# A two-layer decoder trunk on one core: the first pair of tiles of each feed-forward by eight plain products, the sums of input blocks made beside them

## The chip, the cores and the metric

The kernel runs on one core of a Trainium2 chip. The metric is the device time of one execution in microseconds (us); the times given are medians of several runs. TensorE (PE) multiplies, VectorE (DVE) and ScalarE (ACT) do the work element by element, GpSimd (POOL) issues the DMAs that add into their target, and SyncE (SP) issues all the others.

## The reference

512 positions of width 1024 pass through two layers. Each layer is a feed-forward, a mixer (attention and a short convolution) and a second feed-forward, so the program has four feed-forwards, called FFN1 to FFN4 here. Everything is float32. The change touches the feed-forwards alone:

```python
D_MODEL = 1024
SEQ = 512
DEPTH = 2
D_FF = 2816
...
def _swiglu(h, w1, w2):
    g, up = jnp.split(h @ w1, 2, axis=-1)
    return (jax.nn.silu(g) * up) @ w2
...
        x = x + 0.5 * gate[:, 0] * _swiglu(ada(x, 0), ffn_w1[layer, 0], ffn_w2[layer, 0])
        x = x + gate[:, 1] * _mixer(ada(x, 1), w_in[layer], q_norm_g[layer], k_norm_g[layer],
                                    conv_w[layer], conv_b[layer], w_out[layer])
        x = x + 0.5 * gate[:, 2] * _swiglu(ada(x, 2), ffn_w1[layer, 1], ffn_w2[layer, 1])
```

`ada` is an RMS norm with a scale and a shift that a linear map of `c` gives (the "ada" rows: a product of a 128x1024 weight tile with `c`, 144 of them in all, done on VectorE between other work).

## The kernel before

**Precision.** A float32 product is made of three TensorE products. Every weight tile is split into `whi` (a copy by ScalarE, L167) and `wlo` (the rest, by VectorE, L168), every input into a high and a low half (L512, L513), and `shared_bulk` (L277 to L281) issues whi·hhi, whi·hlo and wlo·hhi as matmuls of 256 columns (L280). The split weights lie in a ring of four (tags `whi`, `wlo`): a fifth split waits until the matmuls of the first are done.

**W1 by blocks.** The first matrix of a feed-forward has 22 gate tiles and 22 up tiles; they go in NP = 11 pairs, pair n being two gate tiles and two up tiles of 128 columns. The input is cut in four blocks, two halves of the sequence by two kinds of 128-row chunks (even and odd), and the weights of a pair in four blocks b11, b12, b21, b22. A plain product of a pair takes eight block products; here every pair is done by seven, numbered in the order 1, 2, 5, 6, 7, 4, 3. For that, sums are needed. Those of weight blocks are made on the way: `left` is negated by ScalarE (L215), added to by VectorE (L218, L221) and by an accumulating DMA on POOL's queue (L179). Those of input blocks, t1 to t4, are made once per feed-forward by the class `Blocks` (scale L432, shift L455, combine L473, split L512 and L513); products 5, 6, 7 and 4 need t1, t2, t3 and t4, product 3 needs the second half of the odd chunks itself. Products 1 and 2 need only the first half of the sequence. One block product is 24 matmuls: four chunks k, two tiles f, three matmuls each.

**Banks.** The results come out of PSUM by `evacuation` (L623 to L668): a copy on ScalarE (L638), additions on VectorE (L633), silu on ScalarE (L629), the product of gate and up (L648), which is split and put into the tiles `hidh`, `hidl` of a pool that opens only when the tiles of the work before are released.

**Order.** `_ffn_order` (L88) writes it out by hand: (1 and 2 of pair 0), (1 and 2 of pair 1), (2, 1), (2, 2), then 5, 6, 7 of pairs 0 and 1 in turn, (0, 4), (0, 3), (1, 4), (1, 3), then a steady pattern; W2 comes in three parts, the first after 32 block products ("the first stretch"). The steps of the input sums are queued as `steps`, each with a number of matmul columns after which it is issued (`after`, `tick`); a product that needs one not yet issued issues it first. `Feed.step` holds that loop:

```python
                while p > 2 and (p, k // 2) not in Tail.blocks[0].made:
                    steps.pop(0)[1]()
```

Weights are loaded and split ahead by `fetch`, two ahead of the product that uses them. The end of the part before a feed-forward (`Tail.run`) computes the norm of the two sequence halves one after the other, and queues `early` (the first half) and t1 to t4 (the second). FFN1 has no part before it: `side_by_side` starts it by running the four products (0,1), (0,2), (1,1), (1,2) chunk by chunk beside the ada products that give its scale and shift.

## Time and profile before

| | |
|---|---|
| time, three runs | 1901.28, 1901.44, 1902.0 us, median 1901.44 |
| the profiled execution | 1905.03 us, of which the span of the trace is 1903.2 |
| PE busy | 1832.5 us, 96% of the span |
| weight loads (PEld) | 1699.7 us, 89%, beside the matmuls |
| DVE, ACT, POOL busy | 1442.6, 944.2, 88.5 us |
| mean granted TensorE clock | 0.991 of full speed |

The profiled execution is 3.6 us longer than the median of the timed runs. In the trace, "PE" rows of L280 are the block products. A number in brackets at a row's end is the time that the engine stood idle just before that row, and behind the arrow stands what it waited for. The first L280 matmuls of the four feed-forwards start at 24.84, 618.61, 976.88 and 1552.43 us.

### The profile page before, as it was taken

To read this page: it belongs to the slowest core of one execution; us is meant where nothing else is said; L and a number is where in the kernel's file an instruction comes from. 1 tells how busy PE (TensorE), PEld (TensorE's weight loads), DVE (VectorE), ACT (ScalarE), POOL (GpSimd) and SP (SyncE) were. 2 spreads that over 40 slices of the span, in tenths; PEclk is the share of its full clock that TensorE was granted. 3 is DMA by queue.
4 is the path that set the end of the run, shared out by engine and by line. 5 is a ranking of instruction groups with operands and counts; after the bars stand their busy time and mean duration, and the time that the engine had idled before them with its cause. 6 is when DMAs were issued, how large, how long until landed. Compare 5 with 4: busy or idle time off the path is not lost.

```text
span 1903.2 us, 31033 instructions
## 1 busy us (share of the span) xinstructions
PE 1832.5 (96%) x12340; PEld 1699.7 (89%) x12340; DVE 1442.6 (76%) x2458; ACT 944.2 (50%) x1482; POOL 88.5 (5%) x164
## 2 busy tenths in 40 slices
PE   4899999999999899999989999999999998999999
PEld 3898999999888898998889999898998898989898
DVE  7896887787866997878779777866977768647564
ACT  4652543446664752542565435344656656436342
POOL 0100000000000000000001000000000001000000
PEclk9899999999999999999999999999999999999999
DMA  8687785522314488777607866723222327626422
GB/s 336 188 242 256 207 244 176 155 76 71 102 67 133 98 247 266 194 229 240 211 23 212 243 201 175 244 67 100 84 73 89 107 72 187 168 89 165 134 60 85
DMA packets 86277, 300.52 MB, mean 158 GB/s; under 512 B 9458, under 2 KB 10482, under 8 KB 86132
## 3 DMA queue, kind: packets, MB, share of 16 engines
q1 hardware_dynamic: 73460, 252.40, 38.7%
q0 software_dynamic: 12672, 46.14, 14.0%
q8 instruction: 97, 1.59, 0.3%
q14 instruction: 48, 0.39, 0.1%
HBM read 296.41 MB, written 2.10 MB: 157 GB/s over the span
## 4 chain that ended last, share of the span: by engine, by line
PE 56%; DVE 3%; ACT 2%; DMA 1%; issue 1%; ACTq 0%; POOLq 0%
PE acc L280 27%; PE acc L273 9%; PE acc L274 9%; PE acc L275 9%; DMA left<-in_w 1%; ACT whi L167 1%; DVE h L513 1%; PE acc L830 0%; DVE wlo L168 0%; PE tp L821 0%; PE tp L851 0%; ACT tv L455 0%; ACT ev L638 0%; ACT h L512 0%; DVE sum L218 0%
## 5 line engine op out<-in xcount | busy, mean ns | idle before, releaser
L280 PE MATMUL acc<-h,whi 128*128 128x256 f32 x4928 | 891.6, 283 | 35.0 <-ACT h L512 18.5
L280 PEld LDWEIGHTS acc<-h,whi 128*128 128x128 f32 x4928 | 766.9, 191 | 41.1 <-ACT h L512 21.8
L280 PE MATMUL acc<-h,wlo 128*128 128x256 f32 x2464 | 694.2, 282 | 9.7 <-DVE wlo L168 9.5
L167 ACT ACTIVATE whi<-raw 128x1024 fp32r<-128x1024 f32 (+1 forms) x300 | 302.8, 1012 | 379.5 <-PE acc L274 226.2
L280 PEld LDWEIGHTS acc<-h,wlo 128*128 128x128 f32 x2464 | 470.2, 191 | 11.2 <-DVE wlo L168 11.2
L168 DVE TENSOR_TENSOR wlo<-raw,whi 128x1024 fp32r<-128x1024 f32 (+1 forms) x300 | 347.3, 1164 | 64.6 <-ACT whi L167 61.4
L273 PE MATMUL acc<-hidh,whi 128*128 128x512 f32 (+1 forms) x776 | 287.1, 370 | 0.0
L275 PE MATMUL acc<-hidh,wlo 128*128 128x512 f32 (+1 forms) x776 | 286.7, 369 | 0.0
L274 PE MATMUL acc<-hidl,whi 128*128 128x512 f32 (+1 forms) x776 | 286.6, 369 | 0.0
L299 DVE SCALAR_TENSOR_TENSOR ada<-ada,cb 128x1024 f32<-128x1024 f32 x144 | 174.2, 1222 | 81.4 <-DMA ada<-in_w_ada 75.1
L529 DVE SCALAR_TENSOR_TENSOR x<-acc,fin,x 128x512 f32<-128x512 f32 (+1 forms) x130 | 87.5, 674 | 129.8 <-PE acc L275 129.5
L275 PEld LDWEIGHTS acc<-hidh,wlo 128*128 128x128 f32 x776 | 146.2, 188 | 24.9
L274 PEld LDWEIGHTS acc<-hidl,whi 128*128 128x128 f32 x776 | 146.3, 188 | 24.5
L273 PEld LDWEIGHTS acc<-hidh,whi 128*128 128x128 f32 x776 | 146.2, 188 | 24.3
L167 ACT ACTIVATE whi<-left 128x1024 fp32r<-128x1024 f32 x88 | 93.1, 1058 | 142.9 <-DMA left<-in_w 82.5
L167 ACT ACTIVATE whi<-sum 128x1024 fp32r<-128x1024 f32 x88 | 93.2, 1059 | 139.7 <-DVE sum L218 92.6
L168 DVE TENSOR_TENSOR wlo<-left,whi 128x1024 fp32r<-128x1024 f32 x88 | 106.9, 1218 | 37.8 <-ACT whi L167 37.1
L273 PE MATMUL acc<-h,whi 128*128 128x512 f32 (+1 forms) x346 | 132.0, 382 | 0.4 <-ACT h L512 0.4
L168 DVE TENSOR_TENSOR wlo<-sum,whi 128x1024 fp32r<-128x1024 f32 x88 | 107.3, 1219 | 30.7 <-ACT whi L167 30.7
L274 PE MATMUL acc<-h,whi 128*128 128x512 f32 (+1 forms) x346 | 126.8, 366 | 1.0 <-DVE h L513 1.0
L275 PE MATMUL acc<-h,wlo 128*128 128x512 f32 (+1 forms) x346 | 127.0, 367 | 0.0
L273 PE MATMUL acc<-whi,h 128*128 128x384 f32 x256 | 88.9, 349 | 4.9 <-ACT h L436 4.9
(122 smaller groups left out, 2171.3 us busy)
## 6 DMA issues: line engine op xcount, KB each, us to landing
ada<-in_w_ada SPq DMA_DIRECT2D x128, 512.0 KB, 4.4
raw<-in_w SPq DMA_DIRECT2D x88, 512.0 KB, 4.4
raw<-in_w2a SPq DMA_DIRECT2D x64, 512.0 KB, 5.1
left<-in_w SPq DMA_DIRECT2D x44, 512.0 KB, 5.3
sum<-in_w SPq DMA_DIRECT2D x44, 512.0 KB, 4.8
sum<-in_w POOLq DMA_DIRECT2D x44, 512.0 KB, 7.4
left<-in_w POOLq DMA_DIRECT2D x44, 512.0 KB, 5.4
raw<-in_w2b SPq DMA_DIRECT2D x32, 384.0 KB, 3.1
```

Source lines behind the costliest of these rows:

```text
L167: nc.scalar.activation(hi, raw, AF.Copy)
L168: nc.vector.tensor_tensor(out=lo, in0=raw, in1=hi.bitcast(F32), op=ALU.subtract)
L273: nc.tensor.matmul(out, a[0], b[0], start=first, stop=False)
L274: nc.tensor.matmul(out, a[0], b[1], start=False, stop=False)
L275: nc.tensor.matmul(out, a[1], b[0], start=False, stop=last)
L280: nc.tensor.matmul(out, p, q, start=first and i == 0, stop=i == 2, skip_group_check=True)
L299: nc.vector.scalar_tensor_tensor(w, w, 1.0, cb, op0=ALU.mult, op1=ALU.mult, accum_out=raw[:, m, j:j + 1])
L513: return nc.vector.tensor_tensor(out=lo, in0=v, in1=hi.bitcast(F32), op=ALU.subtract)
L529: nc.vector.scalar_tensor_tensor(x[j][:, cols], ps, gate, x[j][:, cols], op0=ALU.mult, op1=ALU.add)
```

## The change

Pair 0 of every feed-forward is done by eight plain products, numbered 11 to 14 (first half of the sequence) and 21 to 24 (second half): 11 and 21 use b11, 12 and 22 use b12, 13 and 23 use b21, 14 and 24 use b22. The second four reuse the split weights of the first four (`kept`), so four weight tiles of pair 0 are split in place of seven. Each of four banks takes two products. Pair 1 and all others are done as before; the order is (11, 12), (13, 14), (21, 22), (23, 24) of pair 0, then (1,1) with (1,2), then the steady pattern from pair 1 on. Other effects of the same diff:

- `second` takes the first part of t1: it scales and shifts the second half and splits its two kinds of chunks into slots 6 and 2 of the moving tiles (four splits). t1 to t3 follow `LATER` columns apart; t4, which overwrites slot 6, only when products 23 and 24 are issued (`release`).
- `hold` keeps the splits of pair 1 back until products 21 and 22 (two splits) and 23 and 24 (the rest) are issued, since the four kept weights fill the ring.
- The gated results of pair 0 are split into `hidh`, `hidl` only after the pool opens (`opened`), which is now ahead of (1, 4).
- FFN1 runs 11 to 14 chunk by chunk beside the ada products and 21 to 24 after chunks 1 and 3; four weights instead of two are fetched ahead of it.
- The part before FFN2 and FFN4 (`out`) fetches four weights ahead instead of one, and the ada products are spread over one place fewer in each feed-forward.

```diff
-MOVING = {2: 0, 1: 1, 3: 2, 5: 3, 7: 4, 6: 5, 4: 6}
+MOVING = {2: 0, 1: 1, 3: 2, 5: 3, 7: 4, 6: 5, 4: 6, 11: 1, 12: 0, 13: 1, 14: 0, 21: 6, 22: 2, 23: 6, 24: 2}
...
-    order = [[(0, 1), (0, 2)], [(1, 1), (1, 2)], [(2, 1)], [(2, 2)]]
-    order += [[u] for u in ((0, 5), (1, 5), (0, 6), (1, 6), (0, 7), (1, 7), (0, 4), (0, 3), (1, 4), (1, 3))]
+    order = [[(0, 11), (0, 12)], [(0, 13), (0, 14)], [(0, 21), (0, 22)], [(0, 23), (0, 24)], [(1, 1), (1, 2)]]
     ends = [p0 + n - 1 for p0, n in PARTS]
-    for n in range(2, NP - 2):
+    for n in range(1, NP - 2):
...
+        if which > 10:
+            return load(src[which - 11])
...
-        if key[0] != "w1":
+        if key[0] != "w1" or key[4] > 10:
             return halves(key, raw, n)
...
+    hold = [len(order)]
...
-        for i in range(len(fetched), min(upto, len(order))):
+        for i in range(len(fetched), min(upto, hold[0])):
...
-        def t1(self, rb, two):
+        def second(self, rb, two):
...
-                if i == 0:
-                    self.combine(t, b12, self.first[two][:, :, 1])
+                self.put(two, 21 + i, v)
+            self.late[two] = b12, b22, half_kb("t").rearrange("p (k n) -> p k n", k=2)
+            self.made.update((p, two) for p in (21, 22, 23, 24, 3))
+
+        def t1(self, two):
+            b12, b22, t = self.late[two]
+            self.combine(t, b12, self.first[two][:, :, 1])
             self.put(two, 5, t)
...
-            self.put(two, 3, b22)
...
-            fetch(used[0] + 4 - SPLIT)
+            fetch(used[0] + (4 if key[0] == "out" else 4 - SPLIT))
...
-                    after(two * LATER, lambda two=two: blocks.t1(r[1], two))
-                for step in (blocks.t2, blocks.t3, blocks.t4):
+                    after(EARLY, lambda two=two: blocks.second(r[1], two))
+                for step in (blocks.t1, blocks.t2, blocks.t3):
                     for two in range(2):
-                        after(LATER // 2, lambda step=step, two=two: step(two))
+                        after(LATER, lambda step=step, two=two: step(two))
...
+            elif p in (12, 22):
+                sums_of[n, p] = half_kb("ev")
+                nc.scalar.activation(sums_of[n, p], banks.pop((n, BANKS[p])), AF.Silu)
+            elif p in (14, 24):
+                hidden(n, p // 20, sums_of.pop((n, p - 2)), banks.pop((n, BANKS[p])))
...
+                if p == 11:
+                    hold[0] = used[0] + 4
+                self.ws.append(kept.pop(p) if p > 20 else weights("w1", l, which, n, p))
+                if 10 < p < 20:
+                    kept[p + 10] = self.ws[-1]
...
+    def release(last):
+
+        if last:
+            hold[0] = len(order)
+            for two in range(2):
+                after(LATER, lambda two=two: Tail.blocks[0].t4(two))
+        else:
+            hold[0] += 2
+        fetch(used[0] + (AHEAD if last else 2))
...
-        groups = _ffn_order()[:2]
-        feeds = []
+        plain_groups = _ffn_order()[:4]
+        feeds = [Feed(0, 0, h, sum(plain_groups[i:i + 2], []), banks) for i in (0, 2)]
...
-            if k < 2:
-                feeds.append(Feed(0, 0, h, groups[k], banks))
-            for f in feeds:
-                for i in range(k) if f is feeds[-1] and k == 1 else ():
-                    f.step(i)
-                f.step(k)
-            if k > 1:
-                first.t1(rb[:, 256:512], k - 2)
+            feeds[0].step(k)
+            if k % 2:
+                first.second(rb[:, 256:512], k // 2)
+                feeds[1].step(k - 1)
+                feeds[1].step(k)
```

The order of the instructions on PE in FFN2, before: behind the fourth product of pairs 0 and 1 (`acc_6644`) come (2,1) and (2,2), from `acc_6726` and `acc_6767`, and then (0,5), the first that needs an input sum.

```order
L280 MATMUL acc_6644<-h_6285,whi_6537 128x256 x2
L280 MATMUL acc_6644<-h_6285,wlo_6538 128x256
L280 MATMUL acc_6726<-h_6284,whi_6634 128x256 x2
L280 MATMUL acc_6726<-h_6284,wlo_6635 128x256
...
L280 MATMUL acc_6767<-h_6284,whi_6640 128x256 x2
L280 MATMUL acc_6767<-h_6284,wlo_6641 128x256
...
L280 MATMUL acc_6804<-h_6284,whi_6720 128x256 x2
L280 MATMUL acc_6804<-h_6284,wlo_6721 128x256
```

The same place now: behind products 13 and 14 (`acc_6647`) come 21 and 22 (`acc_6704`, with weights that were split already, `whi_6278`), 23 and 24 (`acc_6770`), and then (1,1) of pair 1 (`acc_6835`).

```order
L286 MATMUL acc_6647<-h_6304,whi_6299 128x256 x2
L286 MATMUL acc_6647<-h_6304,wlo_6300 128x256
L286 MATMUL acc_6704<-h_6303,whi_6278 128x256 x2
L286 MATMUL acc_6704<-h_6303,wlo_6279 128x256
...
L286 MATMUL acc_6770<-h_6304,whi_6299 128x256 x2
L286 MATMUL acc_6770<-h_6304,wlo_6300 128x256
L286 MATMUL acc_6835<-h_6303,whi_6761 128x256 x2
L286 MATMUL acc_6835<-h_6303,wlo_6762 128x256
```

Four products that wait for no new weight split stand now where products of pair 2 and the first product on an input sum stood. On DVE in FFN2, before, from the scaling of the second half (`tv`) on, the splits of the weights of pair 2 (`wlo_6635`, `wlo_6641`) stand among the input sums (`t`, `h`):

```order
L432 SCALAR_TENSOR_TENSOR tv_6605<-x3_71,fin02_197,tp_6601 128x256
L168 TENSOR_TENSOR wlo_6635<-left_6521,whi_6634 128x1024
L473 TENSOR_TENSOR t_6606<-tv_6604,hva_6286 128x512
L168 TENSOR_TENSOR wlo_6641<-raw_6532,whi_6640 128x1024
L513 TENSOR_TENSOR h_6284<-t_6606,h_6284 128x2x256
L633 TENSOR_TENSOR ev_6630<-acc_6541,ev_6630 128x512
L432 SCALAR_TENSOR_TENSOR tv_6657<-x4_72,fin02_197,tp_6601 128x256
```

The same place now:

```order
L438 SCALAR_TENSOR_TENSOR tv_6622<-x7_75,fin02_208,tp_6600 128x256
L479 TENSOR_TENSOR t_6620<-tv_6606,hva_6305 128x512
L520 TENSOR_TENSOR h_6303<-tv_6606,h_6303 128x2x256
L479 TENSOR_TENSOR tv_6606<-tv_6606,tv_6607 128x512
L520 TENSOR_TENSOR h_6303<-tv_6607,h_6303 128x2x256
...
L520 TENSOR_TENSOR h_6303<-t_6620,h_6303 128x2x256
L170 TENSOR_TENSOR wlo_6762<-left_6288,whi_6761 128x1024
L520 TENSOR_TENSOR h_6304<-t_6635,h_6304 128x2x256
L479 TENSOR_TENSOR tv_6621<-tv_6621,tv_6622 128x512
L170 TENSOR_TENSOR wlo_6767<-raw_6290,whi_6766 128x1024
```

All eight scalings and the input splits come first there; the weight splits of pair 1 (`wlo_6762`, `wlo_6767`) follow behind. On ACT in FFN1, where pair 1 runs, the split of the next pair's `left` and of pair 1's `left` (which waits for the accumulating DMA on POOL's queue) now stand ahead of a silu, of t2's input splits (`t_305`, `t_444`) and of a bank's copy (`ev_666`):

```order
L169 ACTIVATE whi_597<-left_522 128x1024
L169 ACTIVATE whi_635<-left_501 128x1024
L642 ACTIVATE ev_591<-ev_591 128x512
L169 ACTIVATE whi_668<-raw_595 128x1024
L219 ACTIVATE left_522<-left_522 128x1024
L519 ACTIVATE h_200<-t_305 128x2x256
L519 ACTIVATE h_201<-t_444 128x2x256
L169 ACTIVATE whi_702<-raw_630 128x1024
L519 ACTIVATE h_200<-tv_291 128x2x256
L169 ACTIVATE whi_736<-raw_503 128x1024
L651 ACTIVATE ev_666<-acc_530 128x512
```

Before, the input splits stood ahead of the `left` splits there:

```order
L512 ACTIVATE h_190<-t_385 128x2x256
L512 ACTIVATE h_189<-tv_332 128x2x256
L512 ACTIVATE h_190<-tv_383 128x2x256
L167 ACTIVATE whi_507<-sum_414 128x1024
L167 ACTIVATE whi_547<-sum_417 128x1024
L167 ACTIVATE whi_579<-left_111 128x1024
L629 ACTIVATE ev_466<-ev_466 128x512
L167 ACTIVATE whi_609<-left_242 128x1024
```

The weight splits of `left` have moved ahead of input splits that PE needs for products 6 and 7.

## Rows read from the trace of the kernel before

**Rows 1.** The page: span, busy times, share of the span, instructions.
```profile
span 1903.2 us, 31033 instructions
PE 1832.5 (96%) x12340; PEld 1699.7 (89%) x12340; DVE 1442.6 (76%) x2458; ACT 944.2 (50%) x1482; POOL 88.5 (5%) x164
```

**Rows 2.** PE's waits: waited for, us in total, times, longest us.
```profile
PE acc L280 <- ACT h L512: 18.5, 7, 5.3
PE acc L280 <- ACT ev L638: 10.4, 7, 3.4
PE acc L280 <- DVE wlo L168: 9.5, 5, 3.1
```

**Rows 3.** Stretches of L280: length, PE and PEld busy, clock, DMA share, GB/s.
```profile
187.90:267.08 79.18, 79.14 (x672) 79.10 (x672) 1.00 0.76 213
24.80:58.70 33.90, 22.56 (x116) 20.96 (x117) 0.90 0.86 297
24.80:144.38 119.58, 102.81 (x768) 100.47 (x768) 0.94 0.79 238
618.60:720.54 101.94, 94.25 (x768) 92.89 (x768) 0.97 0.64 181
976.87:1078.18 101.31, 96.09 (x768) 94.56 (x768) 0.96 0.62 172
1552.42:1651.71 99.29, 93.88 (x768) 92.50 (x768) 0.98 0.56 148
```

**Rows 4.** The same view: eight products behind the fourth, in FFN2, FFN3 and FFN4.
```profile
630.93:661.46 30.53, 25.55 (x194) 24.94 (x193) 0.89 0.49 110
991.14:1021.64 30.50, 25.49 (x194) 24.34 (x193) 0.94 0.47 109
1564.96:1595.17 30.21, 25.21 (x194) 24.39 (x193) 0.94 0.49 111
```

**Rows 5.** Timeline of PE in FFN2, FFN3: start, us, instruction, idle before.
```profile
641.75 0.50 PE L280 MATMUL acc<-h,whi 128*128 128x256 f32 x2 [1.72 <-ACT whi L167]
645.30 0.58 PE L280 MATMUL acc<-h,wlo 128*128 128x256 f32 x1 [3.05 <-DVE wlo L168]
703.49 0.50 PE L280 MATMUL acc<-h,whi 128*128 128x256 f32 x2 [2.28 <-ACT ev L638]
1005.41 0.39 PE L280 MATMUL acc<-h,wlo 128*128 128x256 f32 x1 [2.55 <-DVE wlo L168]
```

**Rows 6.** Clock behind such waits: all engines busy, then clock, DMA share, GB/s.
```profile
643.86:650.68 6.82, 5.38 (x25) 5.38 (x26) 6.82 (x9) 3.15 (x4) 0.86 (x1) 0.50 0.55 94
```

**Rows 7.** Timeline of DVE, ACT and POOL: the work of one step each.
```profile
625.69 1.66 DVE L432 SCALAR_TENSOR_TENSOR tv<-x,fin,tp 128x256 f32<-128x256 f32 x4 [0.62 <-PE tp L413]
642.23 1.28 DVE L513 TENSOR_TENSOR h<-tv,h 128x512 fp32r<-128x512 f32 x2
682.56 3.49 DVE L168 TENSOR_TENSOR wlo<-raw,whi 128x1024 fp32r<-128x1024 f32 x3
923.75 1.99 ACT L167 ACTIVATE whi<-raw 128x1024 fp32r<-128x1024 f32 x2
60.78 1.15 ACT L512 ACTIVATE h<-tv 128x512 fp32r<-128x512 f32 x2
1007.74 0.86 POOL L179 DMA_DIRECT2D left<-in_w  x1 [5.01 <-DVE sum L218]
1013.35 1.06 ACT L167 ACTIVATE whi<-left 128x1024 fp32r<-128x1024 f32 x1 [3.63 <-DMA left<-in_w]
```

**Rows 8.** Timeline of DVE and PE in FFN1.
```profile
18.32 1.22 DVE L299 SCALAR_TENSOR_TENSOR ada<-ada,cb 128x1024 f32<-128x1024 f32 x1
21.01 1.23 DVE L168 TENSOR_TENSOR wlo<-left,whi 128x1024 fp32r<-128x1024 f32 x1
50.82 1.44 PE L280 MATMUL acc<-h,whi 128*128 128x256 f32 x5 [4.10 <-ACT h L512]
```

**Rows 9.** PE's waits in FFN1 from 58.70 to 144.38.
```profile
PE acc L280 <- ACT ev L638: 5.1, 2, 3.4
```

More of the change, by code (lines that the diff above doesn't have):

```diff
@@ L83, in _units @@
                             yield ("w2", l, which, p, j), src, 2 * PARTS[p][1] * 128
-                    else:
+                    elif u[1] < 20:
                         yield ("w1", l, which, *u), t["w1"][l, which, u[0]], D
 def _ffn_order():
-    order = [[(0, 1), (0, 2)], [(1, 1), (1, 2)], [(2, 1)], [(2, 2)]]
-    order += [[u] for u in ((0, 5), (1, 5), (0, 6), (1, 6), (0, 7), (1, 7), (0, 4), (0, 3), (1, 4), (1, 3))]
+    order = [[(0, 11), (0, 12)], [(0, 13), (0, 14)], [(0, 21), (0, 22)], [(0, 23), (0, 24)], [(1, 1), (1, 2)]]
     ends = [p0 + n - 1 for p0, n in PARTS]
-    for n in range(2, NP - 2):
+    for n in range(1, NP - 2):
         order += [[(n, 5)], [(n, 6)]]
@@ L473, in combine @@
             nc.vector.tensor_tensor(out=out, in0=a, in1=b, op=ALU.subtract)
-        def t1(self, rb, two):
+        def second(self, rb, two):
             b12, b22 = [self.pool.tile([128, S], F32, name="tv", tag="tv", bufs=4)
                         .rearrange("p (k n) -> p k n", k=2) for _ in range(2)]
-            t = half_kb("t").rearrange("p (k n) -> p k n", k=2)
             for i, v in enumerate((b12, b22)):
@@ L484, in t1 @@
                     self.shift(v[:, k], v[:, k], j)
-                if i == 0:
-                    self.combine(t, b12, self.first[two][:, :, 1])
+                self.put(two, 21 + i, v)
[4 more added lines that the diff above has]
+            self.combine(t, b12, self.first[two][:, :, 1])
             self.put(two, 5, t)
-            self.late[two] = b12, b22, t
             self.made.add((5, two))
@@ L506, in t4 @@
             self.put(two, 4, t)
-            self.put(two, 3, b22)
             self.made.add((4, two))
-            self.made.add((3, two))
     def split(hi, lo, v):
@@ L626, in evacuation, with opened @@
         hid = {}
+        waiting = []
+        def opened():
+            while waiting:
+                in_halves(*waiting.pop(0))
         def silu(v):
@@ L640, in hidden, with in_halves @@
         def hidden(n, half, gate, up):
+            v = half_kb("hid")
+            nc.vector.tensor_tensor(out=v, in0=up, in1=gate, op=ALU.mult)
+            if hid_pool:
+                in_halves(n, half, v)
+            else:
+                waiting.append((n, half, v))
+        def in_halves(n, half, v):
             if n not in hid:
@@ L644, in hidden @@
                 hid[n] = [hp.tile([128, 2, S], F32R, name=m, tag=m, bufs=PARTS[0][1]) for m in ("hidh", "hidl")]
-            v = half_kb("hid")
-            nc.vector.tensor_tensor(out=v, in0=up, in1=gate, op=ALU.mult)
             a, b = [z[:, :, HALVES[half]] for z in hid[n]]
@@ L666, in done @@
                 sums_of.pop((n, 2))
-        return banks, done, hid
-    BANKS = {1: "a", 6: "a", 7: "a", 4: "a", 2: "b", 5: "c", 3: "c"}
+            elif p in (12, 22):
[3 more added lines that the diff above has]
+                hidden(n, p // 20, sums_of.pop((n, p - 2)), banks.pop((n, BANKS[p])))
+        return banks, done, hid, opened
+    BANKS = {1: "a", 6: "a", 7: "a", 4: "a", 2: "b", 5: "c", 3: "c",
+             11: 11, 12: 11, 13: 21, 14: 21, 21: 12, 22: 12, 23: 22, 24: 22}
+    kept = {}
     class Feed:
@@ L678, in __init__ @@
             for n, p in group:
-                self.ws.append(weights("w1", l, which, n, p))
-                if p in (1, 2, 5):
+                if p == 11:
[3 more added lines that the diff above has]
+                    kept[p + 10] = self.ws[-1]
+                if p in (1, 2, 5, 11, 13, 21, 23):
                     banks[n, BANKS[p]] = acc_bank()
@@ L685, in step @@
             for (n, p), w in zip(self.group, self.ws):
-                while p > 2 and (p, k // 2) not in Tail.blocks[0].made:
+                while (2 < p < 10 or p > 20) and (p, k // 2) not in Tail.blocks[0].made:
                     steps.pop(0)[1]()
@@ L698, in feed @@
             done(n, p)
+        if group[-1][1] > 20:
+            release(group[-1][1] == 24)
+    def release(last):
[3 more added lines that the diff above has]
+                after(LATER, lambda two=two: Tail.blocks[0].t4(two))
+        else:
+            hold[0] += 2
+        fetch(used[0] + (AHEAD if last else 2))
     def ffn(l, s, h, carried, groups=()):
@@ L705, in ffn @@
         pool = []
-        banks, done, hid = evacuation(l, which, pool)
+        banks, done, hid, opened = evacuation(l, which, pool)
         todo = _ffn_order()
@@ L710, in ffn @@
             groups[0](banks, done)
-        while todo[0][0] != (0, 4):
+        while todo[0][0] != (1, 4):
             feed(l, which, h, todo.pop(0), banks, done)
@@ L716, in ffn @@
         pool.append(stack.enter_context(tc.tile_pool(name="hid", bufs=1)))
+        opened()
         for at, group in enumerate(todo):
@@ L957, in trunk @@
     lead[:] = 0, 0, 0
-    fetch(2)
+    fetch(4)
     for half in range(2):
@@ L986, in side_by_side @@
             first.early(rb[:, 0:256], k)
-            if k < 2:
-                feeds.append(Feed(0, 0, h, groups[k], banks))
-            for f in feeds:
-                for i in range(k) if f is feeds[-1] and k == 1 else ():
-                    f.step(i)
-                f.step(k)
-            if k > 1:
-                first.t1(rb[:, 256:512], k - 2)
-        lead[:] = AHEAD, LOADED, SUMS
-        for n, p in groups[0] + groups[1]:
-            done(n, p)
+            feeds[0].step(k)
[3 more added lines that the diff above has]
+                feeds[1].step(k)
+        lead[:] = AHEAD, LOADED, SUMS
+        for step in (first.t1, first.t2, first.t3):
+            for two in range(2):
+                after(LATER, lambda step=step, two=two: step(two))
+        for group in plain_groups:
+            for n, p in group:
+                done(n, p)
+        release(True)
         late_constants()
-        for step in (first.t2, first.t3, first.t4):
-            for two in range(2):
-                after(LATER // 2, lambda step=step, two=two: step(two))
-    groups = (side_by_side, 2)
+    groups = (side_by_side, 4)
     for l in range(DEPTH):
```

## The prediction

> **What bounds the kernel now.** I read the page first, then PE's waits, then PE's block products stretch by stretch, then the timelines of the engines where PE waits. The page [rows 1] shows PE busy 96% of the span, DVE 76%, ACT 50%: as a whole PE is the bound, and 24 matmuls more on it should cost time. The waits [rows 2] say where PE isn't: L280 waits 18.5 us for input splits, 10.4 for bank copies, 9.5 for weight splits. The stretches [rows 3] place them. In the steady pattern 672 matmuls, 28 block products, take 79.15 us with PE busy throughout: 79.15/28 = 2.827 us a product. At that price the 32 products of a first stretch are 90.46 us. They take 119.58, 101.94, 101.31 and 99.29 in FFN1 to FFN4: 29.1, 11.5, 10.85 and 8.8 us are lost. These 60.3 us are all that the change can win; the second and third stretches have next to nothing to give.
>
> In FFN2 to FFN4 most of the loss lies in eight products behind the fourth [rows 4]: 30.53, 30.50 and 30.21 us for 8 x 2.827 = 22.6, so 7.9, 7.9 and 7.6 lost. The timeline [rows 5] shows how: PE stands 1.72 and 3.05 us at 641.75 and 645.30 (2.55 at 1005.41 in FFN3), since ACT and DVE have to make, in the same 15 us, the second half of the input, its sums and the splits of a new weight for each product. Behind these waits the granted clock is 0.50 for 6.82 us [rows 6], so each matmul there takes twice as long; about half of PE's busy time of that window, some 3 us, belongs to the loss too. Outside these eight, FFN2 to FFN4 lose about 3.6, 3.0 and 1.2 us, one 2.28 at 703.49 for a bank copy [rows 5] among it.
>
> **What the change costs.** Eight plain products take the place of seven: one product more in each feed-forward, 4 x 2.827 = **+11.3 us** on PE, with nothing to hide it. It takes off DVE three weight splits (1.14 each, three in 3.49 [rows 7]), two weight sums of the same size and three bank additions, off ACT three splits (0.95), a negation and three copies; it adds two input splits on each (0.60 on DVE, 0.52 on ACT). That is some 6 us of DVE and 4 of ACT in each feed-forward. Beside full PE this is worth nothing; it counts only in the start, where PE waits for these two engines.
>
> **FFN2 to FFN4.** Now the four products of the first half end where four did before, at 630.93, and behind them stand 48 matmuls for products 21 to 24 whose weights are split already. They need the second half: eight scalings from 625.69, 0.40 each, and four splits [rows 7]. Putting these rows in the new order of DVE, the four low halves are there at 630.1, 631.3, 633.1 and 634.3, each just ahead of the matmuls that read it. So the eight plain products end at 630.93 + 4 x 2.83 = 642.3. The two splits released by 21 and 22 (ring slots free at 636) end on DVE at 638.5 and 640.8: 1.5 us ahead of need. DVE then makes t1 to t3 while PE runs (1,1), (1,2), (1,5), (1,6), 2.83 each: the low half of (1,5) is ready at 644.4 for 648.0, that of (1,6) at 649 for 650.8. The next is `left` for (1,7): its sum is done on DVE at 646.1, POOL's DMA is issued 0.65 later and lands 5.6 behind that (1007.74 to 1013.35 [rows 7]), at 652.3; ACT then has, in its order, four pieces of a weight's size (0.95), a silu and a bank copy of about 0.5 each: 4.8 us, so 657.1, against PE at 656.5. I take 0.65 us of wait. That is the sum for each of the three: lost before 7.9, 7.9, 7.6; less the additional product 2.83 and this 0.65: **−4.4, −4.4, −4.1 us**. Bounds: no wait at all gives 0.65 more each; a wait as the largest of today, 3.05 with a half-clock window of 3 us behind it, takes 5.5 each. I stand near the lower end, because the margins above come from rows and each is positive but the last. The start (norm and transposes) and the 2.28 wait are left as they are.
>
> **FFN1.** Here DVE sets the pace at the start by the ada products; PE stands 4.10 us at 50.82 for a split of the first half [rows 8]. From 21.01 on [rows 8] its queue up to the last split of the second half is four weight splits x 1.14, twelve ada products x 1.15, sixteen scalings x 0.40, eight input splits x 0.60 and 1.3 of small rows: 30.9 us, so about 52. Behind it 48 matmuls are left, 5.66 us at full clock and some 1.2 more for what PE starts with at half clock after such a wait: the eight plain products end at 58.8. Before, PE had 116 matmuls done by 58.70, 4.8 products [rows 3]; so the new order is 3.2 products ahead, of which one is the additional one. Then it gives back. Before, the remaining 652 matmuls, 27.2 products or 76.8 us, took 85.68: 8.9 lost, 5.1 of it for bank copies [rows 9] and the rest half clock. Now 25 products, 70.7 us, follow, and the weights of pair 1 could not be split ahead (the ring of four holds the kept ones). Putting ACT's rows in the new order, pair 1 waits seven times, 1.4 for its (1,1) input split and 0.4 to 2.6 behind ACT's split of `left`, which stands ahead of t2's input splits and of a copy: 9.5 us in sum, by 94. I add 1.7 for a bank copy as at present (5.1 less 3.4 [rows 9]) and 1.5 for half clock: 83.4 us. 58.8 + 83.4 = 142.2 against 144.38: **−2.2 us**. Bounds: without the seven waits −11.7; with twice as long ones +7.3. I keep the middle, since most of these waits hang on one DMA landing.
>
> **The sum.** −2.2 − 4.4 − 4.4 − 4.1 = −15.1 us: the profiled execution, 1905.0, becomes 1890, and the median 1901.4 becomes **1886** (the profiled execution is 3.6 us above the median, in its span and around it; I carry the difference over).
>
> The rows show one engine at 96% and stretches on it without a gap [rows 1, 3]; products added to a full stretch cost their full price. The Trainium skill, "Perfetto Trace Analysis", section "Identifying the Most-Contended Engine", tells to optimize the most-contended engine first, and to judge TensorE by its weight-load share (89% here), not by its busy share. By it, adding four products to relieve DVE and ACT goes the wrong way and the time would be 1901.4 + 11.3 = 1912.8. The section "Optimization Strategy" bears the other way: find the gaps on that engine in its regime, and what blocks it there. The trace has both, and the gaps of the first stretches, 60.3 us, are larger than the price.
>
> **Rivals.**
> *Slower: the waits move to pair 1.* The split of pair 1's weights can't begin until 21 to 24 free the ring; if the margin of 1.5 us is not there, (1,1) and (1,2) wait for splits just as (0,5) does now, each wait brings its half-clock window, and t1 to t3 with their splits then meet the weight splits again. PE would lose as much as before, and the additional products come on top: 1901.4 + 11.3 = **1912.8**. It becomes slower than before from 15.1 us more of waits than I counted, 3.8 in each feed-forward. For it: before, ACT and DVE were late in this same place with a ring that was free. Against it: 6 us of DVE's work are gone and 11 us of PE's work need no new weight.
> *More waiting, but not all.* Pair 1 costs FFN1 its gain (its waits reach 12 us), and FFN2 to FFN4 have one wait of 1 to 2 us with half clock more: −15.1 + 2.2 + 3 x 2 to 3 x 3 = −7 to −4: **1894 to 1897.5**.
> *Less waiting.* The seven waits of FFN1 vanish for the larger part (−7 to −9.5), the 0.65 too: **1874 to 1880**. For it: DVE is relieved, and clock windows that I count as half go with the waits.
> *It does nothing.* PE's gain in the gaps and the additional product balance: 1901; needs the waits at 12 to 18 us above mine, so it is only the seam of the slower rival.
>
> **How the numbers follow.** About 0.2% (3.8 us) is what a measurement of this kernel can tell from no change. Forecast, 1883 to 1891: 0.55. Less waiting, 1874 to 1883: 0.18. More waiting, 1891 to 1897.6: 0.14. Within 0.2%: 0.04. Slower: 0.09. Faster is the sum of the first three, 0.87. The range 1876 to 1897 leaves out the last two and the edges of the others, some 0.18.
>
> **What would show it.** In the changed kernel's trace the first stretch holds 792 matmuls. Right: it takes about 97.5, 97 and 95 us in FFN2 to FFN4 and 117 in FFN1; behind the fourth product, 96 matmuls (products 21 to 24) in 11.3 us at clock 1.00; the first L286 wait of over 0.5 us in FFN2 stands at (1,7), for `whi` or a bank copy; FFN1's eighth product ends near 58.8 and its waits stand behind that, on ACT's splits. Wrong: waits of `wlo` at (1,1) or (1,2) with a clock of 0.50 (the slower rival); a second half that comes later than its matmuls, so that 21 to 24 wait for `h`; or a loss in the second stretch, which the change shouldn't touch (79.15 us for 672).

## The result and the profile after

The changed kernel takes 1891.45 us (median of six runs, 1888.49 to 1893.54) against 1902.74 of the kernel before (six runs, 1901.28 to 1905.53): a ratio of 0.9938, 95% interval 0.9925 to 0.995, which is 11.8 us less (9.5 to 14.3). Forecast were 15.1 us less and 1886, range 1876 to 1897. The profiled execution took 1890.81 us, its span is 1889.0.

The page of the changed kernel, beside [rows 1]: PE is busy for 1.7 us more in all with 96 matmuls more, DVE, ACT and POOL have less to do.

```profile
span 1889.0 us, 31142 instructions
PE 1834.2 (97%) x12436; PEld 1702.1 (90%) x12436; DVE 1418.1 (75%) x2434; ACT 925.2 (49%) x1462; POOL 81.6 (4%) x156
```

PE's waits in the block products of the whole changed kernel (waited for, us in total, times, longest us), beside [rows 2]: of the waits for weight splits (`wlo`, 9.5 us) 0.4 are left; those for input splits fell by 2.5 us and those for bank copies by 2.1. Waits for a bank's addition on DVE went from 1.3 us, none of it in FFN2's first stretch, to 2.9, of which 1.7 lie there.

```profile
PE acc L286 <- ACT h L519: 16.0, 7, 5.7
PE acc L286 <- ACT ev L651: 8.3, 8, 2.5
PE acc L286 <- DVE ev L646: 2.9, 2, 1.7
PE acc L286 <- DVE wlo L170: 0.4, 2, 0.2
```

The first stretches of FFN1 to FFN4 (window, length, PE busy, weight loads busy, granted clock, DMA share, GB/s), now with 792 matmuls, beside the 768 of [rows 3]:

```profile
25.07:142.97 117.90, 104.42 (x792) 100.80 (x792) 0.96 0.72 223
616.21:716.36 100.15, 94.92 (x792) 93.73 (x792) 1.00 0.53 145
969.93:1068.02 98.09, 97.00 (x792) 96.12 (x792) 0.97 0.51 140
1542.15:1637.59 95.44, 94.38 (x792) 93.60 (x792) 1.00 0.48 122
```

Against 119.58, 101.94, 101.31 and 99.29 they are 1.7, 1.8, 3.2 and 3.9 us shorter, 10.5 together, although each holds a product more. The span fell by 14.2. Of the rest, 2.8 us is the third stretch of FFN2, which took 50.87 us in the trace of before (2.3 of it waits for bank copies) and 48.1 to 48.2 in the thirteen other traces, of the old order and the new: a matter of that one execution, and not a gain. Another 1.0 us is FFN1's second stretch, 78.1 in place of 79.2, at a faster pitch of the same matmuls (told at the end).

The heart of the change, behind the fourth product of FFN2 to FFN4, where [rows 4] had 30.2 to 30.5 us for eight products. Products 21 to 24:

```profile
628.99:640.29 11.30, 11.30 (x98) 11.30 (x97) 1.00 0.01 1
985.06:996.36 11.30, 11.30 (x98) 11.30 (x97) 1.00 0.00 0
1554.94:1566.24 11.30, 11.30 (x98) 11.30 (x97) 1.00 0.01 1
```

PE is busy for the whole of it in all three, at a granted clock of 1.00 (two matmuls more than 96 are cut by the windows' edges). The waits of [rows 5] at 641.75 and 645.30 and the half clock of [rows 6] are not there. The next four products, (1,1), (1,2), (1,5) and (1,6), take 11.31 us in FFN2, also without a wait: the splits of pair 1 come in time.

FFN1 up to the end of its eight plain products, and from there to W2:

```profile
25.08:59.62 34.54, 29.38 (x192) 28.16 (x193) 0.90 0.86 313
59.62:142.97 83.35, 75.04 (x602) 72.63 (x600) 0.98 0.67 185
```

Forecast were an end of the eight products at 58.8, and 83.4 us behind it.

In FFN2, PE's waits in the timeline of the changed kernel (start, duration, instruction, idle time before and what ended it):

```profile
654.99 0.50 PE L286 MATMUL acc<-h,whi 128*128 128x256 f32 x2 [0.40 <-ACT ev L651]
...
697.34 0.50 PE L286 MATMUL acc<-h,whi 128*128 128x256 f32 x2 [2.51 <-ACT ev L651]
707.77 0.50 PE L286 MATMUL acc<-h,whi 128*128 128x256 f32 x2 [1.69 <-DVE ev L646]
```

The first is (1,7), forecast as 0.65. The second answers to the 2.28 at 703.49 of [rows 5], which was to stay. The third has no counterpart in the first stretch of FFN2 in the trace of before. On DVE, just ahead of it, an ada product stands for its load:

```profile
703.61 1.23 DVE L305 SCALAR_TENSOR_TENSOR ada<-ada,cb 128x1024 f32<-128x1024 f32 x1 [3.14 <-DMA ada<-in_w_ada]
```

### The profile page after: what moved, and what is told of

Read it like the earlier page. It is cut to its first block, busy times and chain, and to the rows that moved or that the text cites. A ratio compares the mean times of both kernels' runs of the same rounds, so it can differ in the third digit from the quotient of the medians.

```text
span 1889.0 us, 31142 instructions
## 1 busy us (share of the span) xinstructions
PE 1834.2 (97%) x12436; PEld 1702.1 (90%) x12436; DVE 1418.1 (75%) x2434; ACT 925.2 (49%) x1462; POOL 81.6 (4%) x156
## 3 DMA queue, kind: packets, MB, share of 16 engines
q0 software_dynamic: 11520, 41.95, 12.9%
## 4 chain that ended last, share of the span: by engine, by line
PE 81%; DVE 5%; ACT 3%; DMA 2%; issue 2%; ACTq 0%; DVEq 0%; POOLq 0%
PE acc L286 35%; PE acc L279 14%; PE acc L280 14%; PE acc L281 14%; DMA left<-in_w 2%; DVE wlo L170 1%; DVE h L520 1%; PE acc L873 1%; ACT whi L169 1%; PE tp L864 1%; PE tp L894 1%; DMA ada<-in_w_ada 1%; PE acc L904 0%; PE acc L905 0%; DVE p L908 0%
## 5 line engine op out<-in xcount | busy, mean ns | idle before, releaser
L170 DVE TENSOR_TENSOR wlo<-raw,whi 128x1024 fp32r<-128x1024 f32 (+1 forms) x304 | 352.5, 1166 | 52.9 <-ACT whi L169 49.9
L280 PE MATMUL acc<-hidl,whi 128*128 128x512 f32 (+1 forms) x776 | 286.9, 370 | 0.0
L280 PEld LDWEIGHTS acc<-hidl,whi 128*128 128x128 f32 x776 | 146.4, 189 | 24.3
L169 ACT ACTIVATE whi<-sum 128x1024 fp32r<-128x1024 f32 x80 | 84.8, 1061 | 147.0 <-DVE sum L222 100.7
L169 ACT ACTIVATE whi<-left 128x1024 fp32r<-128x1024 f32 x80 | 84.7, 1058 | 122.7 <-DMA left<-in_w 79.2
L170 DVE TENSOR_TENSOR wlo<-left,whi 128x1024 fp32r<-128x1024 f32 x80 | 97.7, 1221 | 52.6 <-ACT whi L169 52.1
L280 PE MATMUL acc<-h,whi 128*128 128x512 f32 (+1 forms) x346 | 126.9, 367 | 1.0 <-DVE h L520 1.0
L170 DVE TENSOR_TENSOR wlo<-sum,whi 128x1024 fp32r<-128x1024 f32 x80 | 97.7, 1221 | 32.5 <-ACT whi L169 32.3
```

The lines of the kernel that those rows point to most:

```text
L169: nc.scalar.activation(hi, raw, AF.Copy)
L170: nc.vector.tensor_tensor(out=lo, in0=raw, in1=hi.bitcast(F32), op=ALU.subtract)
L280: nc.tensor.matmul(out, a[0], b[1], start=False, stop=False)
```

## The experiments

A time is given with its ratio to the kernel before and the 95% interval of that ratio. Differences of less than about 2.5 us between two variants can't be told from these intervals.

**What a product costs.** The kernel before, with (6,5) of each feed-forward issued twice; the first pass is thrown away.

```diff
-        for k in range(KD // 2):
+        for k in range(KD // 2) if group != [(6, 5)] else [*range(KD // 2)] * 2:
             f.step(k)
```

> The kernel before, with product (6, 5) of every feed-forward issued twice (the second pass opens the bank anew, so the first is thrown away): four products of 24 matmuls more, in a stretch where PE has no gap. The sum of the prediction takes 2.83 us for each, 11.3 us in all, 1914 us. If a product more gives DVE, ACT or a DMA time that PE would have waited for later in the program, it is less, 1905 to 1910.

1917.59 us, ratio 1.0082 (1.0068 to 1.0095): 15.6 us more (12.9 to 18.1). The stretches that hold the doubled product, in FFN1 and FFN2, and the first stretch of FFN2:

```profile
187.35:269.34 81.99, 81.98 (x696) 81.93 (x695) 1.00 0.70 198
769.14:851.13 81.99, 81.98 (x696) 81.93 (x695) 1.00 0.69 198
620.84:725.58 104.74, 96.84 (x768) 95.29 (x768) 0.95 0.63 177
```

81.99 less the 79.18 of [rows 3] is 2.81: the price in a full stretch is as the sum had it, nothing hides it. The other 4 us or so are not in these stretches. 2.8 of them, in this trace, are in the first stretch of FFN2, ahead of FFN2's doubled product (104.74 against 101.94 of [rows 3]): waits of 0.38 and 2.33 us and a clock of 0.50 behind the second, where before had one of 2.28 with a clock of 1.00 behind it. A run below, without the doubling, shows such a first stretch too, so it varies; whether the doubling has a part in it stays open.

**The reuse of the split weights.** The changed kernel, with 21 to 24 of FFN2 to FFN4 loading and splitting their weights again.

```diff
-                self.ws.append(kept.pop(p) if p > 20 else weights("w1", l, which, n, p))
+                self.ws.append(kept.pop(p) if p > 20 and (l, which) == (0, 0) else weights("w1", l, which, n, p))
...
-                    elif u[1] < 20:
+                    elif u[1] < 20 or (l, s) != (0, 0):
...
```

> The changed kernel, with products 21 to 24 of FFN2 to FFN4 loading and splitting their weights anew instead of reusing those of 11 to 14 (FFN1 as changed): four loads and four splits more in each, 4.6 us of DVE and 3.8 of ACT in the stretch where the second half of the input and its sums are made; the products and their order stay. If the gain comes from PE having work that needs no new split there, the splits of 23 and 24 come about 1.2 us late, the weight sum of pair 1 about 3 us late, and PE loses some 3 us in each of the three, up to 6 with half clock: 1900 to 1909 us. If it comes from the input sums being needed later alone, it is 1891 to 1894.

1899.12 us, ratio 0.9977 (0.9968 to 0.9985): some 7.4 us slower than the changed kernel by the ratios. With the loads and splits come the ring slots that they take, and `hold` is out of use in FFN2 to FFN4. The eight plain products' second half, as above, and the three first stretches:

```profile
630.40:642.99 12.59, 11.58 (x99) 11.38 (x98) 1.00 0.52 168
989.93:1002.72 12.79, 11.54 (x98) 11.20 (x97) 1.00 0.50 165
1561.78:1574.37 12.59, 11.58 (x99) 11.37 (x98) 1.00 0.49 168
...
617.62:721.93 104.31, 97.35 (x792) 95.50 (x792) 0.98 0.57 162
975.49:1074.92 99.43, 96.42 (x792) 94.83 (x792) 0.97 0.57 159
1549.00:1647.22 98.22, 95.30 (x792) 93.85 (x792) 1.00 0.51 140
```

1.3 to 1.5 us are lost in the second half itself, as forecast (1.2), and the three stretches are 4.2, 1.3 and 2.8 longer, 8.3 together. So the work without a new load and split carries the larger part of the gain of 11.8 us; which of the two, the run doesn't separate. It is not all: with the same four splits more on DVE and ACT the kernel still wins 4.4 us over the kernel before, FFN1's part among them, which this run leaves as changed. The loss was below the 9 us or more that I expected. In the windows of the plain products no half clock came: the waits there were of 1.0 to 1.3 us, and the clock is 1.00. Further on in FFN2 one came, 0.50 for 3.4 us from 704.41 on, behind a wait of 2.88 for a bank copy.

**The ring of four.** The changed kernel, with 21 to 24 as one group, so that the ring frees its first slot 2 us before the end of the eight products instead of 5.7.

```diff
-    order = [[(0, 11), (0, 12)], [(0, 13), (0, 14)], [(0, 21), (0, 22)], [(0, 23), (0, 24)], [(1, 1), (1, 2)]]
+    order = [[(0, 11), (0, 12)], [(0, 13), (0, 14)], [(0, 21), (0, 22), (0, 23), (0, 24)], [(1, 1), (1, 2)]]
...
```

> The changed kernel, with the products 21 to 24 of FFN2 to FFN4 issued as one group, chunk by chunk, instead of two groups of two: the same work, but the four kept weights are all in use until the last chunk, so the ring frees its first slot for pair 1 about 2 us before the eight products end instead of 5.7 us before. If the ring decides (my reading: the margin for the splits of (1,1) and (1,2) was 1.7 us in the trace of the changed kernel), PE waits up to 1.3 us for the weight splits of (1,2), the weight sum of pair 1 is made about 1.5 us later and (1,7) waits 1.5 us more; with the half clock behind such waits 3 to 6 us in each of the three, 1900 to 1910 us in all. If the ring does not matter, because DVE and ACT have room there, it stays at 1891.5.

1891.78 us, ratio 0.9946 (0.9933 to 0.9959): no difference that the intervals show. The first stretches of FFN2 to FFN4:

```profile
615.19:715.27 100.08, 95.18 (x792) 93.84 (x792) 1.00 0.52 145
970.11:1068.16 98.05, 96.20 (x792) 95.20 (x792) 0.97 0.51 140
1542.37:1638.58 96.21, 94.64 (x792) 93.70 (x792) 1.00 0.46 121
```

By the stretches only FFN4 is longer, by 0.8 us, but that hides the same loss in all three. The six products behind the plain ones, (1,1) up to (1,7), in FFN2 to FFN4:

```profile
639.28:657.74 18.46, 17.48 (x147) 17.13 (x145) 1.00 0.44 97
995.33:1014.45 19.12, 17.48 (x146) 17.08 (x145) 1.00 0.42 96
1566.45:1584.87 18.42, 17.48 (x146) 17.13 (x145) 1.00 0.43 97
```

They took 17.63, 17.96 and 17.65 us in the changed kernel, so 0.8, 1.2 and 0.8 are lost here, at the places that I had named: (1,1) with (1,2), and (1,7). In FFN3 the first of them waits for a weight split; (1,7) waits 0.94 to 0.98 us in all three.

```profile
996.42 0.39 PE L286 MATMUL acc<-h,wlo 128*128 128x256 f32 x1 [0.70 <-DVE wlo L170]
```

In FFN2 shorter waits further on make up for it, in FFN3 a faster start and pitch. My theory of this run was right on the place and wrong on the size: I expected 3 to 6 us in each of the three. The first two splits of pair 1 end 4.2 and 3.7 us later in FFN2, the margin of 1.5 us is gone, and PE loses about a microsecond in each; the clock stays at 1.00 behind these short waits.

**FFN1 alone.** The changed kernel, with FFN1 in its old order (`_ffn_order` and `side_by_side` of before for the first feed-forward).

```diff
-        todo = _ffn_order()
+        todo = _ffn_order(bool(groups))
...
```

> The changed kernel, with FFN1 in the order of before (seven products for pair 0, chunk by chunk beside the ada products) and FFN2 to FFN4 as changed. My sum gave FFN1 2.2 us of the gain, the two traces 1.7: then it takes 1893 to 1894 us, and the first stretch of FFN1 119 to 120 us. If FFN1's part is worth nothing or costs, 1889 to 1891.

1892.35 us, ratio 0.9932 (0.9918 to 0.9945): by time, FFN1's part can't be told from nothing. The stretch of FFN1 in this trace:

```profile
24.82:145.47 120.65, 101.50 (x768) 98.93 (x768) 0.94 0.78 237
```

In the four traces with FFN1's old order the stretch took 119.1 to 121.7 us (mean 120.2), in the ten with the new one, some of them with ada products elsewhere, 115.9 to 120.0 (mean 117.7). The difference of 2.5 agrees with the 2.2 us of the prediction to within the spread; the traces bear it, the times can't.

**The spacing of the input sums.** The changed kernel with t1 to t4 1024 columns apart, as before.

```diff
-                        after(LATER, lambda step=step, two=two: step(two))
+                        after(LATER // 2, lambda step=step, two=two: step(two))
...
```

> The changed kernel, with the steps t1 to t4 half as many matmul columns apart (1024 in place of 2048), as they were before the change. In FFN1 the input splits of t2 then stand ahead of the splits of left on ACT, so the wait of 2.26 us at (1,6) should go, 1889 us; FFN2 to FFN4 hardly move, as their sums are made early anyway. If the wider spacing was what kept DVE free for the weight sum of pair 1, that sum comes 1 to 2 us later and FFN2 to FFN4 lose as much: 1894 us or more.

1891.34 us, ratio 0.9938 (0.9925 to 0.995): the same. The wait in FFN1 did not go, it was 2.65 us, again for input splits of (1,6), at 72.96 instead of 2.26 at 75.14:

```profile
72.96 0.38 PE L286 MATMUL acc<-h,whi 128*128 128x256 f32 x1 [2.65 <-ACT h L519]
```

The spacing is no part of the gain. The expectation was that these splits would stand ahead of the splits of `left` on ACT; they moved ahead of three other instructions only, and still stand right behind the last split of `left`, which waits for the accumulating DMA:

```profile
71.33 1.06 ACT L169 ACTIVATE whi<-left 128x1024 fp32r<-128x1024 f32 x1 [3.27 <-DMA left<-in_w]
72.30 0.61 ACT L519 ACTIVATE h<-t 128x512 fp32r<-128x512 f32 x1
```

So the run doesn't test what the input splits would do ahead of `left`; its row agrees with the prediction, by which they wait behind it.

**Ada products, where they were.** One place less for them is a side effect of the change, and FFN2's new wait stood behind one. The kernel before with that alone:

```diff
-                if group[0][1] in (7, 3):
+                if group[0][1] in (7, 3) and group[0] != (0, 3):
```

> The kernel before, with one place less for the ada products in each feed-forward (none behind (0,3)), as the change has it, and nothing else changed. If this part of the change costs what the new wait in FFN2 suggests (two ada products at (2,3), the third finds its buffer of two not loaded, DVE waits 3.1 us and a bank's addition comes 1.7 us late), it is 1 to 4 us slower than before, 1904 to 1907 us. If it is only a shift of work with room, it stays within 1 us of before.

1904.94 us, ratio 1.001 (1.0001 to 1.0019): 1.9 us slower, barely clear of nothing. The first stretch of FFN2:

```profile
620.78:725.61 104.83, 96.24 (x768) 94.24 (x768) 0.97 0.62 171
```

2.9 us longer than in [rows 3]; but the run with the doubled product, which has the places of before, had 104.74 there, so the length alone doesn't show that the place is the cause. The rows show more: there is a wait of the new kind, for a bank's addition on DVE behind an ada product that waits for its load. Neither trace with the places of before has one in this stretch.

```profile
689.98 1.23 DVE L299 SCALAR_TENSOR_TENSOR ada<-ada,cb 128x1024 f32<-128x1024 f32 x1 [3.01 <-DMA ada<-in_w_ada]
...
695.29 0.69 PE L280 MATMUL acc<-h,whi 128*128 128x256 f32 x2 [2.69 <-DVE ev L633]
```

The changed kernel, with one ada product at most behind (2,3) and (3,7):

```diff
-                    next_job(max(0, -(-left // places)))
+                    next_job(max(0, min(-(-left // places), 1 if group[0] in ((2, 3), (3, 7)) else 2)))
```

> The changed kernel with one ada product at most at the places behind (2,3) and (3,7), the rest spread over later places. If two ada products in a row at (2,3) are what makes DVE wait for the third one's load, the wait of 1.69 us for a bank's addition in FFN2 goes and with it 1.7 to 2.4 us: 1889 to 1890 us, and the first stretch of FFN2 takes 98 us instead of 100.1. If that wait has another cause, it stays at 1891.5 us and 100.1.

1889.9 us, ratio 0.9931 (0.9918 to 0.9944). FFN1 and FFN2:

```profile
25.10:145.06 119.96, 105.88 (x792) 102.13 (x792) 0.93 0.73 222
619.34:716.66 97.32, 94.31 (x792) 93.32 (x792) 1.00 0.55 152
```

The wait of 1.69 us went and FFN2 came down by 2.8 us, but FFN1 took 2.1 more. With the cap in FFN2 alone:

> The changed kernel, with one ada product at most behind (2,3) and (3,7) in FFN2 alone (FFN1 as changed). In the run with this cap in FFN1 and FFN2 the first stretch of FFN2 took 97.3 us in place of 100.1, and that of FFN1 120 in place of 115.9 to 118.3. If the cap costs FFN1, this gives 1888 to 1889 us; if FFN1's difference was one of executions, 1889 to 1891 as that run did.

1890.72 us, ratio 0.9927 (0.991 to 0.9945), FFN1 at 117.45 and FFN2 at 97.72 us. And with FFN3's five ada products behind its first part of W2 as well:

> The changed kernel, with both places of ada products that helped a first stretch: the cap of one product behind (2,3) and (3,7) in FFN2, and FFN3's five products behind its first part of W2 instead of ahead of it. FFN2's first stretch at 97 to 98 us (100.1 in the changed kernel), FFN3's at 96.8 (98.1), nothing more in FFN1: 3 to 4 us less than the changed kernel, 1887 to 1888.5 us. If the products moved in FFN3 make waits in its later stretches, as in FFN1 with nine more, 1891 or more.

1889.22 us, ratio 0.9924 (0.991 to 0.9938). FFN2 and FFN3:

```profile
616.38:717.88 101.50, 95.63 (x792) 94.25 (x792) 0.98 0.52 145
971.86:1066.22 94.36, 93.76 (x792) 92.96 (x792) 0.98 0.47 121
```

FFN3 is 3.7 us shorter than in the changed kernel, of which some 2 us are a faster pitch of its matmuls (told at the end); FFN2, with the very cap that gave 97.3 and 97.7 before, is at 101.5: a miss. The wait at the capped place is gone there too, but others came, one of 3.05 us for a bank copy with a clock of 0.50 from 699.0 on. These three are the lowest ratios of all, 1.3 to 2.7 us below the changed kernel, and none is clear of its interval.

The changed kernel with three places per pair instead of two, one ada product at each:

```diff
-                if group[0][1] in (7, 3):
+                if group[0][1] in (5, 7, 3):
```

> The changed kernel, with three places for ada products in each pair (behind 5, 7 and 3) instead of two, and one product at each, two at the first. If the waits of FFN2's first stretch (2.51 us for a bank copy, 1.69 for a bank's addition) and of FFN1's (2.38) come from DVE standing at ada products whose load has not landed, they go: first stretch of FFN2 95 to 97 us instead of 100.1, 1886 to 1888 us in all. If they come from the accumulating DMA of left alone, nothing moves: 1891.

1896.76 us, ratio 0.9965 (0.9953 to 0.9978): slower by some 5 us, the opposite of what I expected. DVE's waits for loads of ada tiles (us in total, times, longest us) in the changed kernel:

```profile
DVE ada L305 <- DMA ada<-in_w_ada: 81.6, 66, 5.5
```

With the cap in FFN1 and FFN2:

```profile
DVE ada L305 <- DMA ada<-in_w_ada: 70.2, 65, 4.6
```

With three places:

```profile
DVE ada L305 <- DMA ada<-in_w_ada: 92.0, 73, 5.2
```

FFN1's second stretch took 82.45 us there, in place of the 79.18 of [rows 3]. More places did not mean more time for the loads.

**Ada products taken out of, and put into, a first stretch.** First, FFN2's own gate done in FFN1, and FFN2 and FFN3 without an ada product ahead of the first part of W2:

```diff
             norm(l, 2)
-            if l > 0:
-                gate(l, 2)
+            gate(l, 2)
         elif l + 1 < DEPTH:
-            gate(l, 2)
             norm(l + 1, 0)
...
```

> The changed kernel, with the ada products of FFN2's own gate done in FFN1 and none in the first stretches of FFN2 and FFN3 (theirs start behind the first part of W2); FFN1 has nine more, behind its first stretch. If DVE standing at ada products is what is left of FFN2's loss, its first stretch goes from 100 us to that of FFN4, 95 to 97, FFN3's stays at 97 to 98, FFN1 loses 0 to 3 in its later stretches: 1886 to 1889 us. If the loads of weights and the accumulating DMA are late by themselves, FFN2 stays at 99 to 100 and FFN1's later stretches lose: 1891 to 1895.

1899.83 us, ratio 0.9978 (0.9967 to 0.9989). FFN1's second stretch, and the first of FFN2 and FFN3:

```profile
187.87:278.05 90.18, 82.65 (x672) 80.86 (x671) 0.98 0.75 217
631.53:727.04 95.51, 94.39 (x792) 93.60 (x792) 1.00 0.47 122
980.75:1077.52 96.77, 94.88 (x792) 94.08 (x792) 0.98 0.46 120
```

FFN2 is at the level of FFN4 (95.44): the 4.6 us that it lost more than FFN4 come with its eight ada products (in the changed kernel's trace seven of them run within the stretch, the eighth just behind it). But eight more of them in FFN1 (seven in its second stretch) cost that stretch 11 us against the 79.18 of [rows 3], where PE had no wait. Then the other way, with eight ada products in the first stretch of FFN4, which had none, eight more in FFN3 and sixteen fewer in FFN2:

```diff
-            if l > 0:
-                gate(l, 2)
...
+        else:
+            gate(l, 2)
...
```

> The changed kernel, with the ada products spread the other way: FFN2 and now FFN4 too have eight in their first stretch (two at each of four places), FFN2 none behind that but in the parts, FFN3 eight more than before. FFN4 is the clean place: its first stretch had no ada product and lost 2.2 us. If ada products in a first stretch make the losses, it goes from 95.4 to 97 to 100 us, and the whole to 1892 to 1896. If not, FFN4 stays at 95.4 and the whole at 1890 or below.

1897.56 us, ratio 0.9965 (0.9953 to 0.9977). FFN4:

```profile
1541.41:1639.96 98.55, 94.92 (x792) 93.72 (x792) 1.00 0.51 142
```

3.1 us longer than in the changed kernel (the profiled execution, 1893.17 us, was the fastest of this kernel's ten, so the trace can't tell where the others lost the rest), with two new waits of the kinds of FFN2's, 80 and 90 us into the stretch as there:

```profile
1621.51 0.50 PE L286 MATMUL acc<-h,whi 128*128 128x256 f32 x2 [1.45 <-ACT ev L650]
1631.38 0.50 PE L286 MATMUL acc<-h,whi 128*128 128x256 f32 x2 [1.12 <-DVE ev L645]
```

Both runs together show that the waits of FFN2 which FFN4 doesn't have, 80 and 90 us into the stretch, come with the ada products. Whether their time on DVE or their loads beside the other loads make them is not separated, except where DVE is seen to stand for such a load, as at 703.61 above.

## Why the prediction was right, and where it was off

*The bound and the place of the loss* were right: the 7.6 to 7.9 us of [rows 4] were waits, with the half clock behind them, that go when PE has work whose weights are split already. The three windows of 11.30 us show it, and the run that loads and splits them again gives 7.4 us back.

*The price of a product* was right: 2.81 measured in a full stretch, 2.83 in the sum.

*FFN4*: −4.1 forecast, −3.9 measured, with the wait at (1,7) at 0.41 instead of 0.65.

*FFN3*: −4.4 forecast, −3.2 measured. The term that was off is the start, which I left as it is. The first four products took 15.12 us instead of 14.27, at a mean clock of 0.79 instead of 0.83: the half clock behind the wait at the start lasted a little longer. The wait at (1,7) was 0.73. The ten other traces of the new order had 13.8 to 15.0 there, so this is a matter of the execution.

*FFN2*: −4.4 forecast, −1.8 measured in this pair of traces. The step that was off is "the 2.28 wait are left as they are": the wait stayed (2.51), but a second one of 1.69 us came behind it, where an ada product on DVE waits 3.14 us for its load and the bank's addition stands behind that. I had followed DVE's queue only up to (1,7), and had not costed the place that the ada products lost. That ada products make such waits is shown (FFN2 at 95.51 without them, FFN4 at 98.55 with them). That the lost place brings this one is likely: the kernel before with one place less has such a wait (2.69), the two traces with its own places have none there; the changed kernel's stands again in the runs of the ring and of the spacing (1.54 and 1.65), and in none of the three with the cap. But it is absent in the run with FFN1 alone, and by time the place can't be told from chance: with the cap FFN2 took 97.3, 97.7 and 101.5 us, without it (and with the split weights reused) 98.7 to 101.1, and the order of before 101.9 to 104.8. Part of the miss is the trace of before, which had the shortest of the three stretches of the old order; against 104.7, that of the doubled product, the changed kernel's 100.1 is 4.6 less.

*FFN1*: −2.2 forecast, −1.7 in this pair, about −2.5 over all traces. Both parts of the sum were hit within 1 us, 59.62 for 58.8 and 83.35 for 83.4, but by luck in their terms. In the first, DVE's last split ended at 53.60 and not at 52, and the 1.2 us for a start at half clock, which no row of before gave, did not come: the clock was 1.00 from 46.28 to 59.62. (It came in one other trace, that of the first cap: 0.50 for 3.4 us from 52.84 on.) In the second, four waits between 59.62 and 92 sum to 4.0 us, where I had seven of 9.5; three more of 4.1 us behind them, where I had 1.7, and what half clock takes make up for it.

*The sum* of the first stretches is −10.5 instead of −15.1 and the measured difference −11.8; the misses are FFN2's (2.6), FFN3's (1.2), FFN1's (0.5) and FFN4's (0.2). The 1890 for the profiled execution was met (1890.81) by luck: the 2.8 us that FFN2's third stretch lost in the trace of before were in the 1905.0 that I subtracted from, although I had written that the second and third stretches have next to nothing to give. They are also most of the 3.6 us that I carried over. The median, 1891.45, lies just outside 1883 to 1891, in the band that I gave to "more waiting"; 1.3 us of its distance is the kernel before, 1902.74 now and 1901.44 then.

*The rivals.* The slower one, waits moved to pair 1, did not happen: pair 1's splits came in time, as forecast. The run with 21 to 24 in one group takes the margin of 1.5 us away, and the loss is 0.8 to 1.2 us in each feed-forward, not the 3.8 and more that this rival needs; its premise that each wait brings its half-clock window was wrong, as the clock stayed at 1.00 there. "Less waiting" and "more waiting" both came true in part: pair 1 of FFN1 waited less, FFN2 more. PE is the fullest engine in both kernels and 96 matmuls were added to it, yet the time fell by 11.8 us. The Trainium skill, "Perfetto Trace Analysis", section "Identifying the Most-Contended Engine", tells to optimize the most-contended engine first, and TensorE to be judged by its weight-load share (89% here). What the prediction took from it, that products added to that engine go the wrong way, did not come true. It holds only where a stretch has no gap: there the doubled product costs its full 2.81 us. The same page's section "Optimization Strategy" tells to find the gaps on that engine within the regime. This trace agrees: the 7.6 to 7.9 us of [rows 4] were there.

## What to carry to other kernels

An engine that is 96% busy can take more work and finish earlier, if the work fills a gap in which it waits for others and asks nothing new of them: here the 11.3 us of four products with their weights split already, for the price of one product more, 2.8 us. Look for such a gap stretch by stretch, cost the addition at the full price, and then follow the queues of the relieved engines further than the gap itself, to the next place where side work with a load of its own (here the ada products) stands ahead of something that the full engine needs.

## What the runs showed that I had not expected

The pitch of the same matmuls at the same granted clock has two values. The second half of FFN4's first stretch, the same 379 matmuls with PE busy throughout, in the changed kernel and then in the one with the closer spacing:

```profile
1590.37:1634.77 44.40, 44.40 (x379) 44.40 (x378) 1.00 0.68 169
```

```profile
1591.10:1633.74 42.64, 42.64 (x379) 42.64 (x377) 1.00 0.68 174
```

From one start to the next that is 0.118 and 0.113 us; a product takes 2.83 us or 2.72. From the longer to the shorter it changed only at waits of PE, short ones among them, in some executions and not in others: in the changed kernel FFN1's second stretch has eighteen products in a row at 2.72, behind a wait of 0.34. Back to the longer it went at waits too, but three times with PE busy throughout, as in FFN2 of the first run with the cap, at 635.30. What sets it is open. It is worth up to 2 us a stretch, as much as several of the differences that were looked for here, and it is one reason why a single trace's stretch can't settle them.
